# The second product of every seven-part layer also by four products of whole blocks

## The chip, the cores and the metric

The kernel runs on one core of a Trainium2 chip. The metric is the device time of one execution in microseconds (us); lower is better. Before the change it is 2457.88 us, the median of 3 runs (2457.56 to 2458.41).

## The reference

A decoder trunk of four layers works on 512 tokens of width 1024 in float32. Each layer first mixes tokens (layers 0 and 3 by a short gated convolution, layer 1 by a spatial-gating MLP, layer 2 by retention) and then runs a SwiGLU feed-forward net (FFN) of inner width 2816; each half is preceded by an RMSNorm and added to the residual stream. What the change touches is this much:

```
def short_conv_mixer(h, w_in, conv_w, w_out):
    b_gate, c_gate, z = jnp.split(h @ w_in, 3, axis=-1)
    cz = c_gate * z
    conv = conv_general_dilated(cz, conv_w, ...)      # width 3, causal, per channel
    return (b_gate * conv) @ w_out

def swiglu_ffn(h, w_gate, w_up, w_down):
    return (jax.nn.silu(h @ w_gate) * (h @ w_up)) @ w_down
```

## The kernel before

Activations stand transposed: channels on the 128 partitions, the 512 tokens along the free axis. The residual x is four tiles x0 to x3 of two channel blocks each, so eight blocks of 128 channels. All products of activations and weights are done in split precision: each operand is a high part of type fp32r (names ending in h: xh, wh) and a low part, the residue (xl, wl), and one logical product of two blocks is three matmuls, high by high, high by low and low by high. `split` makes the two parts: a cast on ScalarE (L157) and a subtraction on VectorE (L158). `product` (L166) issues the matmuls (L177) of a list of terms into one PSUM bank, in a fixed order: for all terms but the last the two matmuls with the high weight, then the matmuls with the low weight for these, then the three of the last term.

The layers that this is about are the two convolutions and the four FFNs. I call them seven-part layers, after the form of most of their input products. There, an input product makes two blocks of 128 output channels (a column pair) for all tokens, and it comes in two forms:

- `columns7` (L204) is the seven-part form. The product is looked at as two by two blocks (two output blocks, and for each pair of channel blocks the even and the odd one, with the two halves of the tokens), and made by seven half-size products instead of eight, with sums of blocks on both sides. Each of the 7 parts is 4 terms of 3 matmuls with 256 columns. Four of the seven need sums of weight blocks, four need sums of activation blocks. The parts go to three PSUM banks named after the product with 1, 5 and 2; between parts ScalarE copies a bank (L227, L229, L233) into a small ring "mcp" of four buffers, and VectorE and ScalarE put the result y together (L224, L240, L244). y is a buffer of the ring "tmp", which has three and which also serves the norms and the operand sums.
- `columns4` (L249) is the form of whole blocks. Each of the two output blocks is one PSUM bank, 8 terms of 3 matmuls with 512 columns, from plain weights and plain activations. Two copies on ScalarE (L264) bring it into y, a buffer of the ring "hid", which has six and also holds the hidden blocks.

The weights of a product come in two halves, by one DMA each on the SP queue. `prepare7` (L114) makes what the form needs. With `plain` it splits the 1024 columns of a half as they are (ring "wp"). Without, VectorE adds four sums of blocks (L132 to L134, ring "sums"), three of the plain blocks are split (768 columns, ring "w7") and so are the four sums (1024 columns, ring "wp"). `plan7` puts a product on the list with its form, and `weights` prepares the next product's weights one ahead.

The activations are made by `leave` (L403), the product that ends the layer half before. For each of the 8 output blocks VectorE adds the bank to x (L423); `operand` makes xh on ScalarE (L375) and xl on VectorE (L376); and after each second block `operand_sums` (L382) makes the four sums of the pair: xg on ScalarE (L388), t1 to t4 on VectorE (L392 to L395), and the split th and tl. `squares` (L296) adds up squares for the norm on GpSimd.

Before the change, the first product of each of these layers ("pg" in an FFN, "pc" in a convolution) for the first column pair, m = 0, is in the four-block form; the first convolution, at the kernel's start, does all three of its products for m = 0 so. Everything else is in the seven-part form. The second product is "pu" in an FFN and "pz" in a convolution; a convolution has a third, "pb".

What the engines do in which order is not only the program's order: the framework plans it with a simulated timeline and priorities, and each engine then executes its queue in that order. So matmuls of neighbouring products are mixed, and a matmul at the head of TensorE's queue that isn't ready holds up those behind it.

Of the kernel before, what the change touches and what calls it, by code (L numbers as in the profile page):

```python
# [21 lines left out]
NB = D // P  # L22
# [19 lines left out]
class Kernel:  # L42
# [448 lines left out]
    def ffn(self, i, g, seven):  # L491
        nc = self.nc
        self.r = before = None
        for lo, hi in FF_PARTS if g is not None else LAST_PARTS:
            hid = []
            gate = []

            def gated(y, gate=gate):
                if self.r is None:
                    self.r = self.scale_in_psum()  # L500
                self.normed(y, self.r)
                nc.scalar.activation(y, y, AF.Silu)
                self.normed(y, self.r)
                gate.append(y)

            def upped(y, gate=gate, hid=hid, blocks=1):
                h = self.hid.tile([P, 2 * T], F32R, tag="hid", name="hidh")
                l = self.hid.tile([P, 2 * T], F32R, tag="hid", name="hidl")
                g = gate.pop()
                n = 2 * T // blocks  # L510
                for b in range(blocks):
                    s = slice(b * n, (b + 1) * n)
                    nc.vector.tensor_mul(y[:, s], y[:, s], g[:, s])
                    self.split(y[:, s], h[:, s], l[:, s])
                hid.extend([(h[:, :T], l[:, :T]), (h[:, T:], l[:, T:])])

            for m in range(lo, hi):
                (self.columns7 if m else self.columns4)("pg", gated)
                if before:
                    self.leave(before, g, seven, False)  # L520
                    before = None
                self.columns7("pu", partial(upped, blocks=2) if m == hi - 1 else upped, m == 0)
            before = hid
        self.finish()
        if g is None:
            self.end(hid)
        else:
            self.leave(hid, g, seven)

    def conv(self, j, g, seven, start=False):  # L530
        nc = self.nc
        self.r = None
        cw = self.conv_w
        acts, got = [], []
        def first(y):
            if self.r is None:
                self.r = self.scale_in_psum()
                self.r2 = self.own.tile([P, T], F32, name="r2")
                nc.scalar.activation(self.r2, self.r, AF.Square)
            self.normed(y, self.r2)  # L540
            got.append(y)

        def second(y):
            cz = got.pop()
            nc.vector.tensor_mul(cz, y, cz)
            got.append((cz, y))

        def third(m, y):
            cz, o = got.pop()
            tap = lambda b, k: cw[:, (j * NB + 2 * m + b) * 3 + k : (j * NB + 2 * m + b) * 3 + k + 1]  # L550
            for b in range(2):
                s = b * T
                nc.scalar.mul(o[:, s : s + T], cz[:, s : s + T], tap(b, 2))
                for k in (1, 0):
                    d = 2 - k
                    nc.vector.scalar_tensor_tensor(
                        o[:, s + d : s + T], cz[:, s : s + T - d], tap(b, k), o[:, s + d : s + T], ALU.mult, ALU.add
                    )
            self.normed(o, self.r)
            nc.vector.tensor_mul(y, y, o)  # L560
            h = self.hid.tile([P, 2 * T], F32R, tag="hid", name="yh")
            l = self.hid.tile([P, 2 * T], F32R, tag="hid", name="yl")
            self.split(y, h, l)
            acts.extend([(h[:, :T], l[:, :T]), (h[:, T:], l[:, T:])])

        for m in range(NB // 2):
            form = self.columns4 if start and m == 0 else self.columns7
            (form if m else self.columns4)("pc", first)
            if m == 3:
                self.leave(acts[:2], g, final=False)  # L570
            form("pz", second, m == 0)
            if start and m == 0:
                with self.tc.issue_after(self.begun.ins):
                    for k in range(NB // 2):
                        self.operand_sums(k, 0)
                    for k in range(NB // 2):
                        self.squares(self.x[k], nc.gpsimd if k < 1 else nc.vector)
            form("pb", partial(third, m), start and m == 0)
        self.finish()
        self.leave(acts[2:], g, seven)  # L580
# [216 lines left out]
    def run(self):  # L797
        nc, a = self.nc, self.a
        for i in range(DEPTH):
            j, kind = divmod(i, 3)  # L800
            if kind == 0:
                for m in range(NB // 2):
                    for part in (1, 2, 0):
                        self.plan7(a["conv_w_in"][j, part * NB // 2 + m], m == 0 and (i == 0 or part == 1))
                        if m == 3 and part == 1:
                            self.plan_out(a["conv_w_out"][j], 0, 2)
                self.plan_out(a["conv_w_out"][j], 2, NB)
            elif kind == 1:
                for q in range(4):
                    for c in range(4):  # L810
                        self.plan(a["sgu_w_v"][j, q, c], 2, T)
                for half in range(2):
                    for m in range(half * NB, half * NB + NB):
                        self.plan(a["sgu_w_u"][j, m], NB, P)
                    for m in range(NB):
                        self.plan(a["sgu_w_out"][j, m, half], NB, P)
            else:
                for hd in range(HEADS):
                    for base in (0, NB):
                        for b in range(2):  # L820
                            self.plan(a["ret_w_qk"][j, base + 2 * hd + b], NB, P)
                    for c in range(4):
                        self.plan(a["ret_w_v"][j, hd, c], 2, T)
                    for e in range(4):
                        self.plan(a["ret_w_g"][j, 4 * hd + e], NB, P)
                    if 0 < hd < HEADS - 1:
                        for m in range(NB):
                            self.plan(a["ret_w_out"][j, m][:, (hd - 1) * VD : hd * VD], VD // P, P)
                for m in range(NB):
                    self.plan(a["ret_w_out"][j, m][:, (HEADS - 2) * VD :], 2 * VD // P, P)  # L830
            for m in range(NF // 2):
                self.plan7(a["ffn_w_gate"][i, m], m == 0)
                for lo, hi in FF_PARTS if i < DEPTH - 1 else LAST_PARTS:
                    if hi == m:
                        self.plan_out(a["ffn_w_down"][i], 2 * lo, 2 * hi)
                self.plan7(a["ffn_w_up"][i, m])
            if i < DEPTH - 1:
                self.plan_out(a["ffn_w_down"][i], *(2 * n for n in FF_PARTS[-1]))
        lo, hi = LAST_PARTS[-1]
# [121 lines left out]
```

## Time and profile before

| | |
|---|---|
| median of 3 runs | 2457.88 us |
| profiled execution | 2457.24 us |
| its span, first to last instruction | 2455.3 us |
| TensorE matmuls in flight | 98% of the span, 14892 matmuls |
| VectorE busy | 76%, 2700 instructions |
| ScalarE busy | 47%, 1638 instructions |
| GpSimd busy | 6% |
| mean granted TensorE clock | 0.995 of full speed |

The busy time of TensorE counts each matmul from its issue to its modelled end, and matmuls overlap; so two starts in a row say more on its pace than the busy share. Idle time is shown in square brackets in the timeline, with what ended it. L followed by a number is a line of the kernel.

### The profile page before, as it was taken

The page shows a single profiled execution, that of the slowest core. Times are in us where ns is not written, and L with a number is a line of the kernel's source. Part 1 is how long each engine was busy: PE and PEld are TensorE (multiplying, and loading weights), DVE is VectorE, ACT ScalarE, POOL GpSimd, SP SyncE. Part 2 cuts the span into 40 slices and gives each one's busy share as a digit, 9 for nine tenths or more (in the row PEclk, how much of TensorE's full clock was granted, in tenths as well). Part 3 has the DMA queues.
Part 4 walks back from the last instruction along what each step waited for, and adds up shares of the span by engine and source line. Part 5 has one row for each costly group of instructions (what it writes and reads, how often), then busy time and mean ns, then how long its engine had stood idle before and what let it go on. Part 6 is the DMA issues. An engine that isn't in the chain of part 4 may idle for free.

```text
span 2455.3 us, 37035 instructions
## 1 busy us (share of the span) xinstructions
PE 2410.1 (98%) x14892; PEld 2174.7 (89%) x14892; DVE 1861.4 (76%) x2700; ACT 1143.3 (47%) x1638; POOL 156.4 (6%) x116
## 2 busy tenths in 40 slices
PE   8999999999999999999999999999999999999998
PEld 7988999988888999998888888799999898889998
DVE  8989878853757988776565465988877898887876
ACT  7555445443324644544333334555435545545443
POOL 1001000020101100002000000200000100100000
PEclk9999999999999999999999999999999999999999
DMA  4241333234332233333323131233234124133331
GB/s 158 89 133 52 116 108 103 90 118 120 95 103 89 78 118 112 95 99 116 95 68 95 61 125 58 93 111 113 87 100 132 52 69 155 52 120 95 95 117 56
DMA packets 78827, 242.05 MB, mean 99 GB/s; under 512 B 8768, under 2 KB 12864, under 8 KB 78656
## 3 DMA queue, kind: packets, MB, share of 16 engines
q1 hardware_dynamic: 77568, 238.65, 31.1%
q8 instruction: 116, 1.90, 0.3%
q10 hardware_dynamic: 1088, 1.05, 0.1%
q14 instruction: 55, 0.45, 0.1%
HBM read 237.56 MB, written 2.10 MB: 98 GB/s over the span
## 4 chain that ended last, share of the span: by engine, by line
PE 90%; DVE 6%; issue 2%; ACT 1%; DMA 1%; POOL 0%; DVEq 0%; SPq 0%; ACTq 0%; POOLq 0%
PE out L177 26%; PE pu L177 21%; PE pg L177 21%; PE pv L177 7%; PE pc L177 3%; PE pb L177 3%; PE pz L177 3%; PE q L177 2%; PE k L177 2%; DVE wl L158 2%; PE po L177 1%; DVE xl L376 1%; PE ps L657 1%; DVE x L423 1%; DVE tl L158 1%
## 5 line engine op out<-in xcount | busy, mean ns | idle before, releaser
L157 ACT CAST wh<-raw 128x768 fp32r<-128x768 f32 (+3 forms) x500 | 426.7, 857 | 610.4 <-PE out L177 197.6
L158 DVE TENSOR_TENSOR wl<-raw,wh 128x768 fp32r<-128x768 f32 (+3 forms) x500 | 491.1, 992 | 135.0 <-ACT wh L157 134.5
L157 ACT CAST wh<-sums 128x1024 fp32r<-128x1024 f32 x208 | 215.1, 1049 | 172.8 <-DVE sums L134 88.6
L177 PE MATMUL out<-hidl,wh 128*128 128x512 f32 (+1 forms) x736 | 278.1, 381 | 0.0
L177 PE MATMUL out<-hidh,wh 128*128 128x512 f32 (+1 forms) x736 | 273.7, 381 | 0.0
L158 DVE TENSOR_TENSOR wl<-sums,wh 128x1024 fp32r<-128x1024 f32 x208 | 250.9, 1220 | 13.4 <-ACT wh L157 9.3
L177 PE MATMUL out<-hidh,wl 128*128 128x512 f32 (+1 forms) x736 | 204.1, 380 | 0.0
L177 PE MATMUL pg<-xl,wh 128*128 128x256 f32 (+1 forms) x672 | 201.0, 315 | 2.5 <-DVE xl L376 2.4
L177 PE MATMUL pg<-xh,wh 128*128 128x256 f32 (+1 forms) x672 | 201.6, 316 | 1.0 <-ACT xh L375 0.8
L177 PE MATMUL pu<-tl,wh 128*128 128x256 f32 x704 | 185.4, 284 | 5.7 <-DVE tl L158 5.7
L177 PE MATMUL pu<-xl,wh 128*128 128x256 f32 (+1 forms) x656 | 188.9, 305 | 0.0
L177 PE MATMUL pu<-xh,wh 128*128 128x256 f32 (+1 forms) x656 | 188.9, 305 | 0.0
L177 PE MATMUL pu<-th,wh 128*128 128x256 f32 x704 | 185.5, 284 | 1.8 <-ACT wh L157 1.7
L423 DVE TENSOR_TENSOR x<-out,x 128x512 f32<-128x512 f32 x192 | 130.3, 683 | 62.7 <-PE out L177 62.5
L177 PE MATMUL pg<-th,wh 128*128 128x256 f32 x640 | 168.0, 283 | 1.6 <-ACT wh L157 1.1
L177 PE MATMUL pg<-tl,wh 128*128 128x256 f32 x640 | 168.0, 283 | 0.0
L132 DVE TENSOR_TENSOR sums<-raw 128x512 f32<-128x512 f32 x208 | 142.1, 694 | 27.9 <-DMA raw<-in_ffn_w_up 24.0
L177 PEld LDWEIGHTS out<-hidl,wh 128*128 128x128 f32 x736 | 138.6, 188 | 24.7
L177 PEld LDWEIGHTS out<-hidh,wh 128*128 128x128 f32 x736 | 138.0, 188 | 24.7
L177 PEld LDWEIGHTS out<-hidh,wl 128*128 128x128 f32 x736 | 136.1, 188 | 26.4
L177 PE MATMUL pg<-xh,wl 128*128 128x256 f32 (+1 forms) x672 | 149.7, 314 | 0.0
L177 PE MATMUL pu<-xh,wl 128*128 128x256 f32 (+1 forms) x656 | 147.4, 304 | 0.0
(265 smaller groups left out, 5733.8 us busy)
## 6 DMA issues: line engine op xcount, KB each, us to landing
raw<-in_ffn_w_gate SPq DMA_DIRECT2D x88, 512.0 KB, 3.6
raw<-in_ffn_w_up SPq DMA_DIRECT2D x88, 512.0 KB, 3.9
raw<-in_ffn_w_down SPq DMA_DIRECT2D x96, 384.0 KB, 3.4
raw<-in_conv_w_in SPq DMA_DIRECT2D x48, 512.0 KB, 4.2
raw<-in_sgu_w_v SPq DMA_DIRECT2D x16, 512.0 KB, 3.6
raw<-in_sgu_w_u SPq DMA_DIRECT2D x16, 512.0 KB, 3.6
raw<-in_sgu_w_out SPq DMA_DIRECT2D x16, 512.0 KB, 3.6
raw<-in_ret_w_qk SPq DMA_DIRECT2D x16, 512.0 KB, 3.6
```

What stands on the lines that cost most here:

```text
L132: nc.vector.tensor_add(sums[:, :2], raw[:, 3:].broadcast_to([P, 2, NB // 4, P]), raw[:, :3:2])
L157: self.nc.scalar.copy(h, src)
L158: self.nc.vector.tensor_sub(l, src, h.bitcast(F32))
L177: nc.tensor.matmul(ps, x, y, start=first and i == 0, stop=last and i == len(seq) - 1, skip_group_check=more)
L376: nc.vector.scalar_tensor_tensor(l[:, s], x[:, s], gm, h[:, s].bitcast(F32), ALU.mult, ALU.subtract)
L423: nc.vector.tensor_add(x[:, s], ps, x[:, s])
L657: nc.tensor.matmul(ps[:, c * P : (c + 1) * P], v[m // 4][c][:, col], ws[grp // 4][:, at], start=True, stop=True)
```

## The change

The first column pair's second product changes from the seven-part to the four-block form: "pu" at m = 0 in all four FFNs, and "pz" at m = 0 in the second convolution (in the first it has that form already). Its weights are planned as plain to match. The loop over FFN parts starts at m = 0 only once per layer. Here is the whole diff:

```diff
@@ ffn
-                self.columns7("pu", partial(upped, blocks=2) if m == hi - 1 else upped, m == 0)
+                (self.columns7 if m else self.columns4)(
+                    "pu", partial(upped, blocks=2) if m == hi - 1 else upped, m == 0
+                )
@@ conv
-            form("pz", second, m == 0)
+            (form if m else self.columns4)("pz", second, m == 0)
@@ run, the plan of the weights
-                        self.plan7(a["conv_w_in"][j, part * NB // 2 + m], m == 0 and (i == 0 or part == 1))
+                        self.plan7(a["conv_w_in"][j, part * NB // 2 + m], m == 0 and (i == 0 or part > 0))
...
-                self.plan7(a["ffn_w_up"][i, m])
+                self.plan7(a["ffn_w_up"][i, m], m == 0)
```

In the plan, part 1 is "pc", part 2 is "pz" and part 0 is "pb". The last argument of both forms, `m == 0`, holds back the work that follows a product's result until the next product is under way.

## Rows read from the trace of the kernel before

**Rows 1.** Part 1 of the page: busy us of each engine, share of the span.
```profile
PE 2410.1 (98%) x14892; PEld 2174.7 (89%) x14892; DVE 1861.4 (76%) x2700; ACT 1143.3 (47%) x1638; POOL 156.4 (6%) x116
```

**Rows 2.** Chain of waits in order of time: start us, us, what.
```profile
20.55 10.88 PE pz L177 x48
...
274.58 1.44 PE pg L177 x12
```

**Rows 3.** Table by stage: stage, its us, busy us and instructions by engine, granted clock, DMA.
```profile
186.80:207.80 21.00, 17.61 (x92) 14.48 (x91) 20.93 (x27) 12.71 (x17) 8.73 (x6) 1.00 0.16 50
813.40:830.40 17.00, 17.00 (x100) 15.09 (x99) 16.93 (x26) 9.70 (x14) 3.61 (x2) 1.00 0.20 63
1555.60:1582.40 26.80, 21.37 (x125) 18.06 (x125) 24.47 (x36) 14.40 (x21) 6.02 (x6) 1.00 0.18 61
1906.70:1930.20 23.50, 18.10 (x85) 15.24 (x84) 20.44 (x30) 13.59 (x17) 10.67 (x6) 0.85 0.15 46
1969.00:1979.00 10.00, 5.83 (x43) 5.43 (x42) 9.16 (x14) 4.04 (x6) 0.00 (x0) 0.95 0.18 54
2090.40:2112.00 21.60, 18.29 (x89) 15.19 (x89) 21.02 (x27) 12.32 (x16) 8.81 (x6) 0.92 0.17 49
```

**Rows 4.** What TensorE waited for: us in total, times, longest.
```profile
PE pu L177 <- DVE tl L158: 5.7, 4, 2.4
PE pz L177 <- ACT th L157: 4.7, 1, 4.7
PE pb L177 <- ACT pbm L229: 4.2, 1, 4.2
...
PE pu L177 <- ACT wh L157: 1.7, 1, 1.7
...
PE pg L177 <- ACT wh L157: 1.1, 1, 1.1
```

**Rows 5.** Groups by form: busy us, mean ns | idle before and its releasers.
```profile
L158 DVE TENSOR_TENSOR wl<-raw,wh 128x768 fp32r<-128x768 f32 x320 | 304.4, 964 | 37.9 <-ACT wh L157 37.4
L158 DVE TENSOR_TENSOR wl<-sums,wh 128x1024 fp32r<-128x1024 f32 x208 | 250.9, 1220 | 13.4 <-ACT wh L157 9.3 <-PE pc L177 3.6 <-PE pg L177 0.5
...
L132 DVE TENSOR_TENSOR sums<-raw 128x512 f32<-128x512 f32 x208 | 142.1, 694 | 27.9 <-DMA raw<-in_ffn_w_up 24.0 <-DMA raw<-in_conv_w_in 3.2
...
L133 DVE TENSOR_TENSOR sums<-sums,raw 128x256 f32<-128x256 f32 x208 | 85.8, 417 | 0.8
...
L157 ACT CAST wh<-sums 128x1024 fp32r<-128x1024 f32 x208 | 215.1, 1049 | 172.8 <-DVE sums L134 88.6 <-PE out L177 33.6 <-PE pg L177 24.6
```

**Rows 6.** Timeline of VectorE, start of FFN 0: start us, us, engine, line, operation.
```profile
186.20 1.44 DVE L158 TENSOR_TENSOR wl<-raw,wh 128x768 fp32r<-128x768 f32 x1
...
203.51 1.78 DVE L376 SCALAR_TENSOR_TENSOR xl<-x,gain,xh 128x512 fp32r<-128x512 f32 x1
```

**Rows 7.** Table by stage, only of "pu" (FFN 0, FFN 2), then of "pz".
```profile
186.80:201.00 14.20, 4.47 (x26) 3.87 (x27) 0.00 (x0) 0.00 (x0) 1.00 0.22 69
1555.60:1570.10 14.50, 1.35 (x10) 1.33 (x10) 0.00 (x0) 0.00 (x0) 1.00 0.00 0
...
1906.70:1918.60 11.90, 2.83 (x12) 2.17 (x12) 0.00 (x0) 0.00 (x0) 0.91 0.22 63
```

**Rows 8.** Timeline of VectorE, start of FFN 2.
```profile
1568.32 1.76 DVE L376 SCALAR_TENSOR_TENSOR xl<-x,gain,xh 128x512 fp32r<-128x512 f32 x1
```

**Rows 9.** Timeline of VectorE, start of the second convolution.
```profile
1918.63 3.02 DVE L376 SCALAR_TENSOR_TENSOR xl<-x,gain,xh 128x512 fp32r<-128x512 f32 x2 [0.52 <-ACT xh L375]
```

**Rows 10.** Timeline of VectorE, ScalarE and TensorE, later in the second convolution.
```profile
1973.39 1.22 DVE L560 TENSOR_TENSOR pby<-pby,pzy 128x1024 f32<-128x1024 f32 x1
...
1976.26 0.75 DVE L224 TENSOR_TENSOR pzy<-pz,pzm 128x256 f32<-128x256 f32 x2
...
1976.77 0.37 ACT L229 COPY pbm<-pb 128x256 f32<-128x256 f32 x1 [1.08 <-DVE pzy L224]
...
1977.19 0.39 PE L177 MATMUL pb<-xh,wh 128*128 128x256 f32 x1 [4.17 <-ACT pbm L229]
```

## The prediction

> **What bounds the kernel now.** I read the page's busy times first: TensorE has matmuls in flight for 98% of the span, VectorE works 76%, ScalarE 47% [rows 1]. A change to this kernel is therefore worth what it adds to or takes from TensorE's own time, and only secondly what it does to the places where TensorE runs dry. The pieces of the chain of waits give TensorE's price at full speed: 48 matmuls of 512 columns in 10.88 us, 226.7 ns each, and 12 of 256 columns in 1.44 us, 120 ns each [rows 2]. With these two prices the table by stage shows where time is lost. Each of its first, second, third, fourth and sixth rows is the start of one seven-part layer that the change touches (FFN 0, FFN 1, FFN 2, the second convolution, FFN 3), from the end of the product before it to about the end of the first product; the fifth is a later place in the convolution [rows 3]. Such a start holds close to 48 matmuls of 512 columns and otherwise short ones, so the time lost is the elapsed time less 10.88 us less 0.12 us for each of the rest:
> - FFN 0: 92 matmuls, 10.88 + 44 x 0.12 = 16.2 of 21.0 us, 4.8 lost;
> - FFN 1: 100 matmuls, 17.1 of 17.0 us, nothing lost;
> - FFN 2: 125 matmuls, 20.1 of 26.8 us, 6.7 lost;
> - second convolution: 85 matmuls, 15.3 of 23.5 us, 8.2 lost;
> - FFN 3: 89 matmuls, 15.8 of 21.6 us, 5.8 lost;
> - the later place: 43 short matmuls, 5.2 of 10.0 us, 4.8 lost.
>
> Together 30.3 us. In the same rows VectorE is busy 20.93 of 21.0, 24.47 of 26.8, 20.44 of 23.5 and 21.02 of 21.6 us: a start is short of operands because VectorE, with ScalarE in front of it, makes them. TensorE's list of waits says which: the sums of activations for the second product (tl, 5.7 us; th, 4.7 us), the second product's sums of weights (wh, 1.7 us), the third product's weights (wh, 1.1 us), and a copy out of PSUM (pbm, 4.2 us) [rows 4]. The granted clock is below 1 in two of the starts (0.85 and 0.92), so part of what they lose is time at the lower of the two levels, 1.2 instead of 2.4 GHz.
>
> **The change, part by part.** Five products change form: "pu" of the first column pair in four FFNs and "pz" of the first column pair in the second convolution. (The first convolution already has this form.)
>
> 1. Columns. A seven-part product is 7 x 12 = 84 matmuls of 256 columns, 84 x 0.12 = 10.08 us; a four-block one is 48 of 512, 10.88 us [rows 2]. TensorE pays 0.80 us more, five times: **+4.0 us**. Nothing hides that, since TensorE is the bound.
>
> The Trainium skill speaks louder against it ("TensorE: Matmul & The Clock Gate", section "Wait — 56ns, not 53.3ns?"): a matmul in a stream costs its columns at 2.4 GHz and about 2.5 ns. By that rule the estimates are 84 x 109.2 = 9.17 and 48 x 215.8 = 10.36 us, 1.19 us more for each product and 5.9 in all. The trace does not agree on the fixed part: both measured prices lie 11 ns above the rule's, which hurts the form with more matmuls, and the sum goes by the measured prices; by the rule it would end 1.9 us later.
>
> 2. Weight preparation. For each of two halves VectorE no longer makes sums (0.694 us and twice about 0.417) nor the second residue (0.964); the one 1024-wide residue stays (1.220) [rows 5]. That is 2 x 2.49 = 5.0 us of VectorE per start, and two casts of ScalarE. At least the residues stand inside the starved stretch: one of 1.45 us at 186.20, while the last half operand of FFN 0 is made only at 203.51 [rows 6]. But the third product's weights will move up into the freed slots and buffers, so I price this relief at 0; its bounds are 0 and the 5.0 us per start where VectorE is full, inside the losses above.
>
> 3. Ready work. This is what I count on. The seven-part form gives TensorE little to do before all activation blocks are there: its parts fill three PSUM banks one after another and several need th and tl. The four-block form needs the plain blocks alone, in two banks, and can take the terms of every block as it comes. In each bank 24 matmuls run in a fixed order: high and low terms of the first seven blocks (14), seven weight residues, the last block's three. Until the last pair of blocks has its low part, 13 per bank can run, 26 x 0.227 = 5.9 us.
> - FFN 0: up to 201 us the old "pu" got through 26 short matmuls, 3.1 us [rows 7]. 2.8 us more work for 4.8 lost: **-2.8**.
> - FFN 3: the same pattern with the same residues and waits, hence the same 2.8: **-2.8**.
> - FFN 2: the one late operand is the low part of the very last block, begun at 1568.32 [rows 8]. All but two matmuls per bank can go before, 44 x 0.227 = 10.0 us against the 10 short ones (1.2 us) that ran [rows 7]. That covers every gap up to there, and the wait for sums of weights (1.7) is gone with the sums. Of 6.7 I leave 1.0 for the third product's weights, which were late already: **-5.7**.
> - Second convolution: at 1918.63 the third pair's low parts are only begun [rows 9]; with two pairs ready, 16 matmuls (3.6 us) take the place of 12 short ones (1.4 us) [rows 7]: **-2.2**. The rest of the 8.2 us stays, since the third pair comes no earlier.
> - FFN 1: nothing was lost, nothing returns: **0**.
>
> 4. Buffers. A seven-part result is put together in the ring "tmp" of three, a four-block result in "hid" of six. In the second convolution "pz"'s first result lives until the gated product reads it for the last time at 1973.39; only after that does VectorE write the next column pair's "pz" (1976.26), only then does the copy pbm find its small buffer (1976.77), and TensorE waits 4.17 us for it [rows 10]. With the first result in "hid" the ring has a free place, and TensorE can go on. I take 4.0 of the 4.8 us lost: **-4.0**; bounds 0 (the next taker of the ring stops in the same way) and 4.8. In "hid" the new tile takes a place that a later hidden block must wait for; the places turn over every product, so I price it at 0, bounds 0 and one elementwise pass a layer, about the 1.2 us of the 1024-wide residue.
>
> 5. Queues. DMAs are the same in number and bytes. ScalarE copies two wide blocks where it copied four narrow ones, beside matmuls. No semaphore wait is added on TensorE; but the order of all engines is planned anew, which moves things by a microsecond or two anywhere.
>
> **Sum.** 4.0 - (2.8 + 2.8 + 5.7 + 2.2 + 4.0) = -13.5 us. The profiled execution took 2457.24 us (span 2455.3 and 1.9 around it), 0.64 below the median of the runs shown, so the forecast is 2443.7 against the profiled run and **2444.4 us** against the median, -0.55%. Hard ends: nothing returns, +4.0, 2461.9; all 30.3 us return, -26.3, 2431.6.
>
> **Rivals.**
> - *The cost eats the gain.* The gaps are fixed by when the last blocks come, and the planner, whose times differ from the chip's, again puts something unready at the head of TensorE's queue: third-product matmuls with th and tl, which the old order also mixed in. Then perhaps a third of the 17.5 us returns: 4.0 - 5.8 = -1.8, 2456. For it: in FFN 0 and the convolution the longest waits are such matmuls of sums [rows 4]. Against it: those were matmuls of the very product that no longer has any.
> - *Slower: the third product's weights.* The third product's sums of weights take the places of the first product's weights, the fourth's those of the second's. Two four-block products that share out the late blocks end late together and free both places late; then a cast of 1.049 and a residue of 1.220 for one half, and a residue for the other, 3.5 us, stand before TensorE can take a sums part [rows 5]. It decides from the point where the first product's last matmul comes less than that before TensorE runs out of the second's. If all five starts pay it and half of the 17.5 returns: 4.0 + 17.5 - 8.8 = +12.7, 2470.6. For it: the wait of 1.1 us for wh by "pg" is this one [rows 4]. Against it: after the last block TensorE still has 22 matmuls in each of the two products, 5 us each, to cover 3.5.
> - *More returns.* VectorE's 5 us and the clock: nearly all of the 30.3, some 2434.
>
> **How the numbers follow.** What a measurement of this kernel tells from no change is about 0.2%, 4.9 us. Forecast and its neighbourhood, 2436 to 2452.9: 0.66. The cost eats the gain, 2453 to 2462.8: 0.20. Slower by the weights' places, above 2462.8: 0.07. More returns, below 2436: 0.07. Faster thus 0.73, same 0.20, slower 0.07. The range runs from 2434 to 2456; it leaves out the slower rival, the upper part of the second case and the lowest ends.
>
> **What would show it.** In the changed profile "pu" matmuls of 512 columns rise by 4 x 48, "pz" ones by 48, and 5 x 84 short ones go. Step 1 is right if the whole is 180 fewer matmuls and the two prices stand. Step 3 is right if TensorE's waits for tl and th by "pu" and "pz" vanish, with no new ones of like size by "pg" or "pb" in the 20 us behind; step 4 if the 4.2 us for pbm are gone and no other copy has them. FFN 1's start should be 0.8 us longer. A wait of "pg" or "pb" for wh or wl of over 2 us in several starts would prove the slower rival; a time above 2456 with the old sum of waits at the starts, the first.

## The result and the profile after

The changed kernel takes 2445.36 us, the median of 6 runs (2442.25 to 2447.57); the kernel before took 2458.14 in the same session. The ratio is 0.9947, 95% interval 0.9934 to 0.9960: 12.8 us or 0.53% less. Its profiled execution took 2447.57 us (span 2445.9), the slowest of the six, so the two traces differ by only 9.4 us in span.

The page of the changed kernel, part 1, the row that answers to [rows 1]:

```profile
PE 2411.2 (99%) x14712; PEld 2165.6 (89%) x14712; DVE 1834.0 (75%) x2645; ACT 1134.2 (46%) x1618; POOL 153.7 (6%) x116
```

180 matmuls fewer, as five products of 84 turned into 48. The chain still has the price of [rows 2] (48 of 512 columns in 10.88 us), and the new products stand among the groups by form (changed kernel, TensorE: x192 where before it was x128, from another layer's "pu"; the 64 are four FFNs of two banks and eight blocks). First the chain, then the group:

```profile
1335.04 10.88 PE q L177 x48
```
```profile
L177 PE MATMUL pu<-xh,wh 128*128 128x512 f32 x192 | 75.2, 395 | 0.0
```

What TensorE waited for in the changed kernel (us in total, times, longest), the list that answers to [rows 4]; the row left out at its top is "pc" for wh, for the most part the wait for the first weights at the kernel's start, 7.1 us before and 7.4 after:

```profile
...
PE pb L177 <- ACT wh L157: 5.4, 3, 4.2
PE pg L177 <- DVE xl L376: 2.3, 4, 0.8
PE pg L177 <- DVE tl L158: 1.7, 2, 0.9
...
PE pg L177 <- ACT th L157: 1.4, 2, 0.7
PE pg L177 <- ACT xh L375: 1.2, 3, 0.7
...
PE pg L177 <- ACT wh L157: 0.5, 2, 0.2
```

The four large entries of before (pu for tl 5.7, pz for th 4.7, pb for pbm 4.2, pu for wh 1.7) are gone. In their place the third product, "pg" or "pb", waits for its own sums, th, tl and wh: smaller in the FFNs, 4.2 us at once in the convolution.

The five starts in the changed kernel, windows in the order FFN 0, FFN 1, FFN 2, second convolution, FFN 3 (columns as in [rows 3]: PE, PEld, DVE, ACT, POOL, granted clock, DMA):

```profile
183.40:204.20 20.80, 17.95 (x74) 13.84 (x74) 19.22 (x27) 14.37 (x18) 5.71 (x5) 0.92 0.30 101
810.00:827.80 17.80, 17.80 (x80) 14.76 (x79) 17.19 (x25) 11.07 (x15) 4.11 (x2) 1.00 0.38 118
1554.80:1578.00 23.20, 21.64 (x93) 16.92 (x92) 23.13 (x32) 13.62 (x18) 6.26 (x6) 1.00 0.29 91
1902.40:1925.00 22.60, 17.65 (x79) 14.38 (x78) 16.80 (x25) 14.28 (x18) 11.52 (x6) 0.92 0.23 69
2082.20:2103.00 20.80, 18.09 (x82) 13.98 (x81) 19.23 (x27) 14.39 (x18) 5.44 (x5) 1.00 0.30 102
```

TensorE without work (window less PE busy) fell in FFN 2 from 5.4 to 1.6 us, in FFN 0, FFN 3 and the convolution only from 3.4, 3.3 and 5.4 [rows 3] to 2.9, 2.7 and 5.0.

For the whole trace I took the distance from each matmul's start to the next, less 226.7 ns (512 columns) or 120 ns (256 columns), and added it up by stage (the first convolution from its second product, 20.5 us, on). This "lost time" includes waits and time at the lower clock. A tenth of a nanosecond on both prices moves the totals by 1.5 us, and their difference by less than 0.1:

| stage | before | after | change |
|---|---|---|---|
| first convolution, to its end | 9.2 | 5.1 | -4.0 |
| FFN 0, start | 4.9 | 6.0 | +1.1 |
| FFN 1, start | 0.0 | 0.0 | 0 |
| FFN 2, start | 6.8 | 2.5 | -4.3 |
| second convolution, start | 8.7 | 6.9 | -1.7 |
| second convolution, rest | 8.5 | 5.5 | -3.1 |
| FFN 3, start | 6.2 | 4.5 | -1.8 |
| whole program | 59.7 | 45.8 | -13.9 |

With the +4.0 of columns that is -9.9 for a span that shrank by 9.4. Half of the time that TensorE ran at a granted clock near 0.5 (1.2 GHz) is lost time: leaving out the last 20 us, there were 17.1 us of it before and 6.8 after, so about 5.1 of the 13.9 is clock. Each row comes from one profiled execution a side; the last section shows how far the row of a start can differ between executions.

The largest entry that the forecast did not have is the end of the first convolution. VectorE there in the kernel before (start us, us, engine, line, operation; in brackets idle time and what ended it):

```profile
162.79 0.69 DVE L132 TENSOR_TENSOR sums<-raw 128x512 f32<-128x512 f32 x1 [3.01 <-DMA raw<-in_ffn_w_up]
163.40 1.22 DVE L158 TENSOR_TENSOR yl<-pby,yh 128x1024 fp32r<-128x1024 f32 x1
```

The same place in the changed kernel:

```profile
161.54 1.23 DVE L158 TENSOR_TENSOR yl<-pby,yh 128x1024 fp32r<-128x1024 f32 x1 [1.12 <-ACT yh L157]
```

Before, the head of VectorE's queue was a weight sum for FFN 0's "pu", which waited 3.01 us for its DMA. Behind it stood yl, the operand of the first convolution's last product. TensorE waited 2.1 us for yl and then ran 3.4 us at half clock. A plain product has no weight sums, so nothing that waits for this DMA stands ahead of yl; its 1.12 us are the wait for its own high part.

### The profile page after: what moved, and what is told of

Same layout as the page of the kernel before. It is cut to its first block, busy times and chain, and to the rows that moved or that the text cites. A ratio compares the mean times of both kernels' runs of the same rounds, so it can differ in the third digit from the quotient of the medians.

```text
span 2445.9 us, 36558 instructions
## 1 busy us (share of the span) xinstructions
PE 2411.2 (99%) x14712; PEld 2165.6 (89%) x14712; DVE 1834.0 (75%) x2645; ACT 1134.2 (46%) x1618; POOL 153.7 (6%) x116
## 4 chain that ended last, share of the span: by engine, by line
PE 91%; DVE 5%; issue 2%; ACT 1%; POOL 0%; DMA 0%; DVEq 0%; SPq 0%; ACTq 0%; POOLq 0%
PE out L177 26%; PE pu L177 21%; PE pg L177 21%; PE pv L177 7%; PE pc L177 3%; PE pb L177 3%; PE pz L177 3%; PE q L177 2%; PE k L177 2%; DVE wl L158 1%; PE po L177 1%; DVE xl L376 1%; PE ps L659 1%; PE ps L177 1%; DVE x L423 0%
## 5 line engine op out<-in xcount | busy, mean ns | idle before, releaser
L157 ACT CAST wh<-sums 128x1024 fp32r<-128x1024 f32 x198 | 205.4, 1049 | 157.0 <-DVE sums L134 86.0
L158 DVE TENSOR_TENSOR wl<-sums,wh 128x1024 fp32r<-128x1024 f32 x198 | 239.0, 1220 | 16.6 <-ACT wh L157 9.4
L177 PE MATMUL pu<-xh,wh 128*128 128x256 f32 (+1 forms) x672 | 201.0, 315 | 0.0
L177 PE MATMUL pu<-xl,wh 128*128 128x256 f32 (+1 forms) x672 | 200.3, 313 | 0.0
L177 PE MATMUL pu<-tl,wh 128*128 128x256 f32 x640 | 168.1, 283 | 0.0
L177 PE MATMUL pu<-th,wh 128*128 128x256 f32 x640 | 167.9, 283 | 0.0
L177 PE MATMUL pu<-xh,wl 128*128 128x256 f32 (+1 forms) x672 | 153.3, 313 | 0.0
L132 DVE TENSOR_TENSOR sums<-raw 128x512 f32<-128x512 f32 x198 | 133.3, 684 | 20.9 <-DMA raw<-in_ffn_w_up 18.5
```

The costliest lines, as they stand in the source:

```text
L132: nc.vector.tensor_add(sums[:, :2], raw[:, 3:].broadcast_to([P, 2, NB // 4, P]), raw[:, :3:2])
L157: self.nc.scalar.copy(h, src)
L158: self.nc.vector.tensor_sub(l, src, h.bitcast(F32))
L177: nc.tensor.matmul(ps, x, y, start=first and i == 0, stop=last and i == len(seq) - 1, skip_group_check=more)
```

## The experiments

All ratios are to the kernel before, with 95% intervals. Edits are shown against the changed kernel unless "before" is named; of each only the main lines stand here, and the plan of the weights, which follows the form, is left out.

**The convolution's result back in the ring "tmp"** (step 4 undone).

```diff
-    y = self.hid.tile([P, 2 * T], F32, tag="hid", ...)
+    y = ring(name + "y") if ring else self.hid.tile(...)
-    (form if m else self.columns4)("pz", second, m == 0)
+    (form if m or start else partial(self.columns4, ring=self.temp))("pz", second, m == 0)
```

> The changed kernel, but the second convolution's first pz result, still made by four products of blocks, is put into the ring tmp of three as before. Theory (the ring held it): TensorE's wait of some 4 us by pb for the copy pbm at about 1970 to 1990 us comes back, and the kernel takes 3 to 5 us more than the changed one (2448 to 2450 against 2445.4). Rival (VectorE, freed of sums, reaches the additions sooner): the wait stays away and the time stays within 1 us of the changed kernel's.

Measured 2446.82 us, 0.9959 (0.9944 to 0.9974). The wait for pbm did not come back; the convolution's rest lost 5.4 us, as in the changed kernel (5.5). VectorE in this run, last reading of the first "pz" result, first writing of the next:

```profile
1955.88 1.22 DVE L562 TENSOR_TENSOR pby<-pby,pzy 128x1024 f32<-128x1024 f32 x1
1960.15 0.41 DVE L224 TENSOR_TENSOR pzy<-pz,pzm 128x256 f32<-128x256 f32 x1
```

Counted from the convolution's start, the last reading comes 55.9 us in, where it came 66.7 us in before (1973.39 in [rows 10]). So in the changed kernel the ring is free in time whether the result lies in it or not. Why the gated product comes ten microseconds earlier was not isolated.

**Before, with only the result moved to "hid"** (step 4 alone).

```diff
-    y = self.temp(name + "y")
+    y = self.hid.tile([P, 2 * T], F32, tag="hid", ...) if hid else self.temp(name + "y")
```

> The kernel before, with one edit: the second convolution's first pz result, still seven-part, is put into the ring hid. Theory (the ring held it): the wait of 4.2 us by pb for pbm goes, 2453 to 2455 against 2458.1. Rival (the load of VectorE): the wait stays and the time with it, 2457 to 2459.

Measured 2454.05 us, 0.9988 (0.9979 to 0.9997). The wait for pbm is gone and the convolution's rest loses 3.9 instead of 8.5 us; the other large waits stay (this run, TensorE's waits):

```profile
PE pu L177 <- DVE tl L158: 5.7, 4, 2.4
PE pz L177 <- ACT th L157: 4.7, 1, 4.7
```

The ring was what held the old kernel there, and another place for the result is one way to free it.

**The old weight work kept** (the change, with the sums and second split still made for the five products, though nothing reads them).

```diff
+                if plain == "load":
+                    sums = self.sums.tile([P, 4, NB // 4, P], F32, tag="sums", ...)
...
+                    h, l = (self.w7.tile([P, 3, NB // 4, P], F32R, tag=part, ...) for part in "hl")
+                    self.split(raw[:, :3], h, l)
```

> The changed kernel, but for the five products VectorE still makes the sums of weights and both engines the second split, and nobody reads them. Theory A (the first convolution's end lost its 4 us to sums at the head of VectorE's queue that waited for the DMA of ffn_w_up): these 4 us come back. Theory B (ready matmuls without sums make the gain in FFN 2 and the second convolution): FFN 2's start still loses only some 2.5 to 3.5 us, and pb's wait for pbm stays away; the whole about 2449 to 2451. Rival (VectorE's relief makes the gain): every start loses as much as before the change and TensorE pays the 4.0 us more, 2458 to 2462.

Measured 2456.20 us, 0.9996 (0.9986 to 1.0005): no gain that can be measured. The loss at the first convolution's end is back (9.0 us), with its wait (VectorE; lines are shifted by the edit, L130 is the sum):

```profile
162.77 0.69 DVE L130 TENSOR_TENSOR sums<-raw 128x512 f32<-128x512 f32 x1 [2.90 <-DMA raw<-in_ffn_w_up]
163.38 1.22 DVE L165 TENSOR_TENSOR yl<-pby,yh 128x1024 fp32r<-128x1024 f32 x1
```

FFN 2's start keeps its gain (2.8 us lost), but 3.6 us of it are lost again just behind, where the casts of sums hold ScalarE and a copy out of PSUM comes late (ScalarE, then TensorE):

```profile
1585.91 1.99 ACT L164 CAST wh<-sums 128x1024 fp32r<-128x1024 f32 x2 [2.13 <-DVE sums L141]
1587.81 0.58 ACT L271 COPY puy<-pu 128x512 f32<-128x512 f32 x1
1588.28 0.37 ACT L234 COPY pgm<-pg 128x256 f32<-128x256 f32 x1
```
```profile
1588.71 0.43 PE L184 MATMUL pg<-th,wh 128*128 128x256 f32 x1 [1.88 <-ACT pgm L234]
```

In all 55.4 us are lost: the new form alone returns 4.3 of the 13.9, about what its columns cost.

**The relief alone** (the kernel before, seven-part, without the weight sums of the five products; plain blocks stand in their places).

```diff
+                if plain == "bare":
+                    out = [out[j] if j < 4 else out[j - 4] + [] for j in range(8)] if half else out
```

> The kernel before with all products seven-part, but for the five products the sums of weights are left out and plain blocks stand in their place, so that only the plain split is made: VectorE and ScalarE are relieved as in the changed kernel, TensorE's matmuls are those of before. Theory A: the first convolution's end gains its 4 us. Theory B (ready matmuls): FFN 2's start still loses 4 us or more because tl, th and the last block are waited for in order, pb's wait for pbm stays, and the time is 2450 to 2454. Rival (relief is all): the starts lose as little as in the changed kernel, and the 4.0 us of columns are saved too, 2440 to 2443.

Measured 2455.48 us, 0.9995 (0.9985 to 1.0004). The end of the first convolution loses 5.1 us, as in the changed kernel. The starts gain little, and FFN 0 and FFN 3 lose more (7.6 each), at a clock of 0.84 in both windows:

```profile
186.50:207.50 21.00, 17.58 (x85) 14.85 (x84) 19.03 (x26) 12.67 (x17) 7.00 (x4) 0.84 0.22 76
2089.00:2110.00 21.00, 17.57 (x81) 14.45 (x80) 19.06 (x26) 11.81 (x17) 6.90 (x4) 0.84 0.27 93
```

56.7 us are lost in all. Relief alone returns 3.0, the form alone 4.3, both together 13.9. What they return only together is clock. TensorE ran at 1.2 GHz for 17.1 us before, 20.5 with the form alone, 23.9 with the relief alone and 6.8 with both. With half of these times taken out, the form alone returns 6.0, the relief alone 6.4 and both 8.7, less than their sum: either one shortens waits, and only with both did the clock fall less often. The mean granted clock over all runs agrees: 0.992 to 0.997 before, 0.995 to 0.996 with the form alone, 0.992 to 0.994 with the relief alone, 0.997 to 0.999 with both.

**FFN 0's product alone.**

```diff
-                (self.columns7 if m else self.columns4)(
+                (self.columns7 if m or i else self.columns4)(
-            (form if m else self.columns4)("pz", second, m == 0)
+            form("pz", second, m == 0)
```

> Of the five products only pu of FFN 0 changes form. Theory (VectorE's queue no longer has sums at its head that wait for the DMA of ffn_w_up): the end of the first convolution loses 5.1 us in place of 9.1, FFN 0's start still loses 4 us or more because the last blocks come 18 to 19 us after it begins whatever the products' form, TensorE pays 0.8; 2453.5 to 2455.5. Rival (the prediction's step 3): FFN 0's start loses 2 us in place of 4.9, and the convolution's end 9.1 as before; 2456.

Measured 2453.53 us, 0.9984 (0.9975 to 0.9993). The end of the first convolution loses 5.1 us and FFN 0's start 6.0, both as in the changed kernel. What this product gains it gains a layer earlier, where VectorE no longer waits for the DMA with a sum, and not at its own start.

**The third product by whole blocks too**, in FFN 0, FFN 3 and the second convolution.

```diff
-                (self.columns7 if m else self.columns4)("pg", gated)
+                (self.columns4 if m == 0 or (m == 1 and i in (0, 3)) else self.columns7)("pg", gated, m == 1 and i in (0, 3))
-            form("pb", partial(third, m), start and m == 0)
+            (form if m else self.columns4)("pb", partial(third, m), m == 0)
```

> The changed kernel, and the third product in the four-block form too in FFN 0, FFN 3 (pg of the second column pair) and the second convolution (pb of the first). Theory A (what these starts still lose is third-product matmuls with th and tl at the head of TensorE's queue): the starts of FFN 0 and FFN 3 lose 2 us or less, the convolution's 4 or less, TensorE pays 2.4 us more; 2438 to 2443. Rival B (the last blocks come when they come, and the ready work runs out): the starts lose within 1 us of what they lose in the changed kernel, and it is slower by the columns, 2446 to 2449.

Measured 2433.91 us, 0.9900 (0.9883 to 0.9916). FFN 0's start loses 1.1 us, FFN 3's 0.8, the convolution's none; 29.5 us in all, and the clock is not halved anywhere but at the end. What was left at these starts was for the most part the third product with its sums. In the changed kernel, of the 4.3 us that FFN 0's start lost at full clock, TensorE stood 2.5 in front of the third product's matmuls with sums and 1.8 in front of "pg" matmuls with plain blocks; the 1.1 us left here are of the second kind. The edit also holds back, by its last argument, the work that follows the second product's result. At the start this is not what acted: in the changed kernel that work first reaches TensorE at 214.7 us, behind the window. Behind the starts, form and holding back were not tried apart.

**Without FFN 1's product.**

```diff
-                (self.columns7 if m else self.columns4)(
+                (self.columns7 if m or i == 1 else self.columns4)(
```

> The changed kernel with FFN 1's pu seven-part again. Its start loses nothing in either form, so only the columns count: 0.8 us less than the changed kernel, 2443.8 to 2445.2 by the median, and the stage from FFN 1's first product to the scale of the next layer is 0.8 us shorter. Rival (a start so short of VectorE needs the relief too): FFN 1's start begins to lose 1 to 3 us.

Measured 2444.91 us, 0.9948 (0.9933 to 0.9963). FFN 1's start loses nothing in either form; the difference to the changed kernel, 0.45 us, has the sign of its columns and is below what a run tells. The stage tells more: from FFN 1's first matmul to the next layer's first it takes 344.25 us here, as in the kernel before, and 345.04 in the changed kernel.

**The sums of activations made later** (without the priority that puts them beside the operands).

```diff
                     self.operand(m, g)
-                    if seven and m % 2:
-                        self.operand_sums(m // 2, g)
+            if final and seven and m % 2:
+                self.operand_sums(m // 2, g)
```

> The changed kernel, with the activations' sums (xg, xt, th, tl) planned without the priority that x, xh and xl have. Theory (xh and xl of the last blocks wait in ScalarE's and VectorE's queues behind the sums, which wait for a buffer that GpSimd holds): the last xl is there 14 us or less after a start in place of 19, the starts of FFN 0, FFN 3 and the convolution lose 1 to 4 us less each, 2436 to 2442. Rival: what is put off comes too late for the third product; its waits for th and tl grow by as much, 2445 to 2452.

Measured 2445.92 us, 0.9950 (0.9935 to 0.9965). The edit moved nothing: through the whole program every engine executes the same instructions in the same order as in the changed kernel. In FFN 0 the last low part on VectorE stands behind the same sum in both and ends 19 us after the start (first the changed kernel, then this run):

```profile
201.40 0.41 DVE L395 SCALAR_TENSOR_TENSOR xt<-xt,xg 128x256 f32<-128x256 f32 x1
201.73 0.74 DVE L376 SCALAR_TENSOR_TENSOR xl<-x,gain,xh 128x512 fp32r<-128x512 f32 x1
```
```profile
200.90 0.42 DVE L395 SCALAR_TENSOR_TENSOR xt<-xt,xg 128x256 f32<-128x256 f32 x1
201.24 0.74 DVE L376 SCALAR_TENSOR_TENSOR xl<-x,gain,xh 128x512 fp32r<-128x512 f32 x1
```

So the theory is untested: whether the last blocks come late because the sums stand ahead of them stays open. What the run does show is how far two executions of one order differ. FFN 0 and FFN 3 lose 6.0 and 4.4 us, unchanged, but the convolution's start loses 4.4 in place of 6.9, and the wait of "pb" for wh falls from 4.2 to 1.6. In front of that wait stands an addition on GpSimd for the norm, and two subtractions on VectorE beside it (the changed kernel, then this run):

```profile
1905.55 4.44 POOL L307 TENSOR_TENSOR sum<-sum,sq 128x512 f32<-128x512 f32 x1 [8.47 <-ACT sq L300]
1905.56 2.08 DVE L158 TENSOR_TENSOR wl<-raw,wh 128x768 fp32r<-128x768 f32 x2
```
```profile
1904.67 1.29 POOL L307 TENSOR_TENSOR sum<-sum,sq 128x512 f32<-128x512 f32 x1 [8.23 <-ACT sq L300]
1904.92 4.08 DVE L158 TENSOR_TENSOR wl<-raw,wh 128x768 fp32r<-128x768 f32 x2
```

Either the addition or the subtractions took long, and which of them differed between executions.

**The third product, and FFN 1 by seven parts again.**

```diff
-                (self.columns7 if m else self.columns4)(
+                (self.columns7 if m or i == 1 else self.columns4)(
...
-                (self.columns7 if m else self.columns4)("pg", gated)
+                (self.columns4 if m == 0 or (m == 1 and i in (0, 3)) else self.columns7)("pg", gated, m == 1 and i in (0, 3))
```

> The kernel with the third product by four products of whole blocks as well (in FFN 0, FFN 3 and the second conv), but FFN 1's second product by seven parts again. Theory A (a product by four products gains only where TensorE would otherwise stand for operands, and costs 0.80 us of columns everywhere): FFN 1's start lost 0 us either way, so this is 0.8 us less than that kernel, 2433.1 us, ratio to before about 0.990, FFN 0, FFN 3 and conv starts still lose about 1 us or less. Rival (FFN 1's relief of VectorE is needed further on): FFN 1 or the scale chain behind it shows waits of over 0.5 us, and the time is 2434.5 us or more.

Measured 2431.73 us, 0.9889 (0.9872 to 0.9905): the quickest version, 27.3 us below before by the ratio. It is 2.2 below the version with FFN 1's product where 0.8 was expected. The profiles show 0.79 for FFN 1's stage and 0.9 less lost in the convolution's rest, 2.6 for 3.5; why is open. The three starts (FFN 0, convolution, FFN 3) in the columns of [rows 3], and TensorE's waits:

```profile
183.40:200.50 17.10, 16.26 (x72) 13.19 (x71) 15.79 (x22) 12.22 (x16) 7.67 (x5) 1.00 0.19 71
1898.30:1918.00 19.70, 19.70 (x88) 16.32 (x87) 19.36 (x27) 15.06 (x19) 6.45 (x5) 1.00 0.27 81
2069.00:2086.00 17.00, 16.55 (x74) 13.39 (x73) 15.69 (x23) 12.34 (x17) 7.23 (x5) 1.00 0.22 75
```
```profile
PE pg L177 <- DVE xl L376: 2.1, 4, 0.8
...
PE pb L177 <- DVE pby L240: 0.8, 1, 0.8
PE pg L177 <- ACT xh L375: 0.8, 1, 0.8
PE pb L177 <- ACT wh L157: 0.6, 1, 0.6
```

TensorE is busy without a gap through the convolution's start, and VectorE in FFN 0 is idle for 1.3 us of the window where it was for 0.1 before [rows 3].

**The third product without the second** (before, with pg and pb as above, every second product by seven parts).

```diff
-                (self.columns7 if m else self.columns4)("pg", gated)
+                (self.columns4 if m == 0 or (m == 1 and i in (0, 3)) else self.columns7)("pg", gated, m == 1 and i in (0, 3))
...
-            form("pb", partial(third, m), start and m == 0)
+            (form if m else self.columns4)("pb", partial(third, m), m == 0)
```

> The kernel before, with only the third product of FFN 0, FFN 3 and the second conv by four products of whole blocks; every second product stays by seven parts. Theory A (the products must be freed of sums from the front, since their matmuls stand in TensorE's queue in order and the second product's th and tl are waited for first): FFN 0 and FFN 3 starts lose 4 to 6 us each as before, the wait for the DMA at the end of the first conv stays at about 3 us, and the time is 2450 to 2457 us. Rival (any product's relief and ready work will do): the starts lose under 2.5 us each and the time is 2438 to 2445 us.

Measured 2458.11 us, 1.0002 (0.9993 to 1.0012). The starts of FFN 0, the convolution and FFN 3 lose 5.1, 9.2 and 6.2 us. VectorE's wait for FFN 0's weights is there again (2.55 us), and TensorE waits in FFN 0 for plain blocks of "pg" and then for the second product's sums:

```profile
195.34 0.51 PE L177 MATMUL pg<-xl,wh 128*128 128x512 f32 x1 [1.46 <-DVE xl L376]
...
200.33 0.39 PE L177 MATMUL pu<-tl,wh 128*128 128x256 f32 x1 [0.69 <-DVE tl L158]
```

The third product alone is worth nothing at the starts and in the time, behind the second it is worth 11.5 us (2445.36 to 2433.91): here the products had to be freed of sums in their order. The reason given in advance is shown only in part. In front of the second product's sums TensorE lost 1.2 us in FFN 0 (3.4 before) and 2.1 in FFN 3; the larger part of FFN 0's loss, 3.8 us, stands in front of plain blocks, and the work that VectorE still does on the second product's weights may be what makes them late. The two were not tried apart.

**The fourth product too** (the quickest version, with FFN 0's and FFN 3's "pu" and the convolution's "pc" at m = 1).

```diff
-                (self.columns7 if m or i == 1 else self.columns4)(
+                (self.columns4 if (m == 0 and i != 1) or (m == 1 and i in (0, 3)) else self.columns7)(
-            (form if m else self.columns4)("pc", first)
+            (self.columns4 if m == 0 or (m == 1 and not start) else form)("pc", first)
```

> The quickest kernel so far (second product by four products of whole blocks but in FFN 1, third product so in FFN 0, FFN 3 and the second conv; 2431.7 us), with the fourth product of FFN 0, FFN 3 and the second conv by four products too. Theory A (the form pays only where TensorE would stand at the start; FFN 0's and FFN 3's starts lose 1.1 and 0.7 us now, the convolution's none): three times 0.80 us of columns and nothing back at the starts, so 2434.1 us, ratio 0.990, unless a part of the 2.6 us that the convolution loses later goes. Rival (the relief of VectorE goes on giving back in the next stages, as it did from the second to the third product): 2430 us or less.

Measured 2432.93 us, 0.9902 (0.9887 to 0.9916), 1.2 above the quickest by the medians and 3.2 by the ratios, where 2.4 was expected; the runs tell no finer. The three starts now lose nothing at all:

```profile
182.50:199.50 17.00, 17.00 (x77) 14.08 (x76) 12.73 (x18) 11.11 (x15) 7.64 (x5) 1.00 0.12 41
...
2065.00:2082.00 17.00, 17.00 (x76) 14.08 (x76) 14.55 (x21) 12.64 (x17) 9.53 (x6) 1.00 0.21 63
```

They gave back what was still lost there (1.1 and 0.7 us), each further product costs 0.80, and the convolution loses 1.2 more later on (3.8 in its rest). With nothing left to return at these starts, a fifth product has nothing to gain there.

**The third product in FFN 2 too** (the quickest version, and FFN 2).

```diff
-                (self.columns4 if m == 0 or (m == 1 and i in (0, 3)) else self.columns7)("pg", gated, m == 1 and i in (0, 3))
+                (self.columns4 if m == 0 or (m == 1 and i in (0, 2, 3)) else self.columns7)("pg", gated, m == 1 and i in (0, 2, 3))
```

> The quickest kernel so far (2431.7 us) with the third product of FFN 2 by four products as well. Theory A (what FFN 2's start still loses, 2.45 us, is two or three waits of the first product for activation blocks that are only being made, 0.71 and 0.93 us and less, and not sums of the third product): the start loses 2.4 us again, the columns cost 0.80, time 2432.5 us. Rival (the third product's load on VectorE is what makes those blocks late): the start loses under 1.5 us and the time is 2431 us or less.

Measured 2433.08 us, 0.9901 (0.9884 to 0.9917); FFN 2's start loses 2.5 us as without it:

```profile
1550.30:1573.00 22.70, 21.09 (x91) 16.47 (x90) 21.33 (x29) 12.85 (x17) 5.22 (x6) 1.00 0.35 107
```

What FFN 2 still loses stands in front of the first product's own blocks (this run):

```profile
1553.68 0.50 PE L177 MATMUL pg<-xl,wh 128*128 128x512 f32 x1 [0.55 <-DVE xl L376]
1556.34 0.72 PE L177 MATMUL pg<-xh,wh 128*128 128x512 f32 x2 [0.76 <-ACT xh L375]
```

The form of the third product does not bring them sooner, although it takes work from VectorE there, 21.33 us busy in the window where the quickest version has 22.63.

## Why the prediction was right, and where it was not

The time came within 1 us of the forecast (2445.36 for 2444.4), and so close a hit is luck: terms that were off by up to 4 us cancelled. What bounds the kernel, the price of the columns and the sign of the change were not luck.

- **What bounds the kernel: right.** All that was gained is TensorE's lost time at starts and waits, less the columns.
- **Step 1, columns: right.** FFN 1 loses nothing in either form, so it shows the price bare: from its first matmul to the next layer's first it took 344.25 us before and 345.04 after, +0.79 for the 0.80 computed. By the Trainium skill ("TensorE: Matmul & The Clock Gate", section "Wait — 56ns, not 53.3ns?") it would have been about 1.19, an estimate. The trace does not agree; the measurement decides for the rows' price.
- **Step 2, relief priced at 0: wrong.** The run with the old weight work kept has no measurable gain. 9.6 of the 13.9 us are lost again without the relief, 3.9 of them at a place that I had not looked at: the weights of FFN 0 are prepared while the first convolution still runs, and there the sums held up its last operand. The bound of 5.0 us per start was right to keep; the choice of its lower end was not, and neither was looking for it only inside the layer that is changed.
- **Step 3, ready work: wrong in FFN 0, FFN 3 and the convolution, right in the main in FFN 2.** Forecast -2.8, -2.8, -5.7, -2.2; found +1.1, -1.8, -4.3, -1.7. Taking out half-clock time, FFN 0 is -0.6, FFN 3 and the convolution are 0: the convolution came near its forecast by the clock alone. The step that failed is "until the last pair has its low part, 13 per bank can run": they could, but TensorE's queue put the third product's sums ahead, 2.5 us in each of FFN 0 and FFN 3. TensorE in the changed kernel, FFN 0:

```profile
194.41 0.50 PE L177 MATMUL pg<-xl,wh 128*128 128x512 f32 x1 [0.84 <-DVE xl L376]
...
198.61 0.38 PE L177 MATMUL pg<-th,wh 128*128 128x256 f32 x1 [0.69 <-ACT th L157]
199.87 0.39 PE L177 MATMUL pg<-tl,wh 128*128 128x256 f32 x1 [0.88 <-DVE tl L158]
```

This is the place that the first rival named. Taking the sums away from the third product took most of the loss away. The rival's time (2456) was wrong since FFN 2, the convolution's rest and the first convolution's end did return theirs.
- **Step 4, buffers: right in size (-3.1 for -4.0), its mechanism not what acted.** Moving the result frees the old kernel, as the run with that alone shows. But the changed kernel doesn't need it: with the result in the ring again the wait stays away.
- **Step 5, queues at 0: wrong in the same way as step 2.** The move past VectorE's queue at the end of the first convolution was worth 4.0 us.
- **The slower rival** (the third product's weights late) happened once, in the convolution. TensorE and ScalarE there, changed kernel:

```profile
1914.64 0.58 PE L177 MATMUL pb<-th,wh 128*128 128x256 f32 x1 [4.18 <-ACT wh L157]
```
```profile
1911.37 1.33 ACT L388 ACTIVATE xg<-x,gain 128x512 f32<-128x512 f32 x2 [5.24 <-POOL sum L308]
1912.61 1.03 ACT L157 CAST th<-xt 128x1024 fp32r<-128x1024 f32 x1
1913.54 1.04 ACT L157 CAST wh<-sums 128x1024 fp32r<-128x1024 f32 x1
```

The cast wh stood on ScalarE behind xg, which waited 5.24 us for GpSimd's sum; it did not wait for a free place, as the rival had it. It took the place of the 4.7 us for th and so cost no more than before. In the run that executes the same order again it was 1.6 us, so its size differs between executions of one order, and the -1.7 of this start is no finer than that.

In sum: forecast -17.5 returned and +4.0 paid; found -13.9 and +4.0 in the profiled executions, -12.8 net between the medians. Of the -13.9, the 4.0 from the first convolution's end made up for most of what FFN 0 and FFN 3 did not give.

## What to carry to other kernels

Free a start of its late operands from the front of the queue: a product without sums gives its gain only if the next product in the in-order queue isn't waiting for the same kind of thing, so change products in order, and stop where a further one brings less than its columns cost. A cheaper preparation has to be priced where it runs, which can be a layer earlier than the product; look at the heads of the queues there. When a change has two effects, try each alone before giving one of them a price of zero, and look at the clock before calling the rest of the gain a joint effect. An edit of priorities tests something only if the engines' order has changed: compare the two timelines first.

## What the runs showed of the hardware

Waits of under 1 us came ahead of a fall of the granted clock: in the changed kernel's FFN 0, after the waits of 0.84, 0.69 and 0.88 us shown above, TensorE ran at 1.2 GHz for 3.4 us from 200.7 us on, 1.7 us lost. FFN 2's waits there (the longest 0.74 us) left it at 1.00, and in the versions that change the third product behind the second it stayed there at all five starts; with the third product changed alone it fell at three of them. A stage's loss in one profile is therefore only good to about 1.7 us: FFN 0's start lost 6.0 us in the changed kernel with such a stretch, and 4.5 without one in the run with the convolution's result back in "tmp", which did not touch that layer. Where GpSimd and VectorE worked side by side the difference was larger: in the second convolution the same addition on GpSimd took 4.44 us in one execution and 1.29 in another of the same order, the two subtractions on VectorE beside it 2.08 and 4.08, and the start lost 6.9 and 4.4 us.
